# Hybrid decoder layer: turn, norm and spread inside the bursts of the next chunk, normaliser rows in another buffer pool, first loads of a recurrence two products sooner

## Chip, core and metric

The kernel runs on one core of a Trainium2 chip. The metric is device time in microseconds (us), from start to end of the program. Engines in the text: PE (TensorE, matmuls and transposes), DVE (VectorE), ACT (ScalarE), POOL (GpSimd) and SP (SyncE, which here issues all DMAs). Each engine works through its own list of instructions in order.

## The reference

One layer on a sequence of 2048 tokens with 1024 channels: a normalised input times one wide weight matrix; four mLSTM heads; two groups of a state-space scan; one output matrix over both; a residual sum and a last norm.

```python
h = rms_norm(x, norm_w[l])
proj = h @ w_in[l]
q, k, v, i_pre, f_pre, o_pre, z_m, z_s, xbc, dt_raw = jnp.split(proj, SPLIT_POINTS, axis=-1)
...
hm = mlstm_chunkwise(q.reshape(Bsz, T, M_HEADS, M_DQK), ...
hm = hm * lax.rsqrt(jnp.mean(hm * hm, axis=-1, keepdims=True) + EPS)
hm = hm.reshape(Bsz, T, M_WIDTH) * mlstm_norm_w[l].astype(f32)
hm = hm * jax.nn.sigmoid(o_pre.astype(f32)) * jax.nn.silu(z_m.astype(f32))
...
y = ssd_chunked(xs, dt, A, ...
y = y + d_skip[l].astype(f32)[:, None] * xs.astype(f32)
y = y.reshape(Bsz, T, S_WIDTH) * jax.nn.silu(z_s.astype(f32))
yg = y.reshape(Bsz, T, S_GROUPS, S_WIDTH // S_GROUPS)
yg = yg * lax.rsqrt(jnp.mean(yg * yg, axis=-1, keepdims=True) + EPS)
y = yg.reshape(Bsz, T, S_WIDTH) * ssd_norm_w[l].astype(f32)
mix = jnp.concatenate([hm, y], axis=-1).astype(dtype)
x = x + mix @ w_out[l]
...
return rms_norm(x, final_norm_w)
```

Both recurrences go in chunks of 128 tokens and carry a state (C for a head, H for a group) from chunk to chunk.

## The kernel before

**Products.** The two large matrix products are cut into 68 jobs. A job multiplies blocks by Strassen's scheme with seven products (R11, R21, T2, T3, T1, R22, T4 by the name of the right operand), and each product is 12 matmuls of 128x512 (L270), since every operand is split into a high and a low part. Two PSUM accumulators run through a job. The copy L289 by ACT takes the accumulator `pa` out after the product T1, and the product R22 then goes on accumulating in it, so R22 cannot start before L289 has ended; one product (R21 of the next job) stands between. Left operands are cast and split by ACT and DVE (L191, L192) a few products ahead. Between jobs of different stages the right operands are refilled from memory (L390).

**Stages and phases.** The input product has two stages (token halves s=0, s=1), each with six phases: heads h0, h1, h2, h3 and groups g0, g1 (order h0, g0, h1, h2, h3, g1; four jobs for a head, five for a group). Two output stages follow. The results of a phase are stored in memory (`hd`, `gd`), and the recurrence of a phase runs while the jobs of the next phase are computed.

**Recurrences.** A head's recurrence has eight chunks. For each chunk: `load` (L676 `hin`, L678 `nmi`, which holds the two rows of the normaliser broadcast to 128 partitions), `scores` (L686 to L704: masks and exponentials E and `w` from `nmi`, transposes of q, k, v on PE into `kw` and `vt`), `memory` (L714 to L735: three matmuls on PE; then square `sj` L731 and copy `mx` L732 on ACT; L733 to L735 on POOL scale `mx`), `gate` (L742 loads `g`) and `turn` (L751 transposes `mx` on PE, L752 multiplies by `g` on DVE, L753 stores to `mix`). A group's recurrence has, for each of its eight chunks, `decay` (L795 to L805), `tokens` (L813 to L829), `states` (L841 to L849), `update` (L857, L862), `outs` (L872 to L883: matmuls on PE, `y` on DVE, `q` on POOL), `norm` (L889 row sum on PE, `r` L891 on DVE, L892 and `dg` L894 on POOL) and `spread` (L901 on PE, L902 on DVE, then a store).

**Order.** PE's order is written by hand: the PE instructions of a recurrence stand in short bursts between two products. After each product `step()` runs: it takes the left operand's next piece, advances a clock by one tick, runs what `later(n, ...)` has put off by n ticks and what `at(...)` has planned, and lets the class Weave decide how many pieces of the recurrence (up to a `yield`) come next, so that NREC pieces are spread evenly over the products of the phase. Before, the turn of a chunk comes four ticks after its memory, the gate one tick after it, norm three and spread five ticks after the outputs. The order on DVE, ACT, POOL and SP is made by a scheduler from this program. `next_w` (from L516 on) prepares the output weights in the background of the second half, 64 pieces planned over 76 ticks; L532 loads a piece and L533 (ACT) scales it.

**Buffers.** Pools of equal buffers are shared by kinds of tiles: r2 (seven buffers: `hin`, `nmi`, `ea`, `xw`, `xdt`, `y`, `z` and others), r1 (six: `vt`, `mx`, `g`), r5 (nine: E, `qp`, `st`, `kw`, `bt`, `cbm`, `q`, `dg`).

Of the kernel before, what the change touches and what calls it, by code (L numbers as in the profile page):

```python
# [69 lines left out]
def hybrid_layer(ctx, tc, x, norm_w, w_in, b_igate, b_fgate, conv_w, conv_b, dt_bias,  # L70
# [30 lines left out]
        return mk([P, 1024], "t", 1, nm)  # L101

    def r2(nm, n=512):
        return mk([P, n], "r2", 7, nm)

    def r1(nm, n=NV):
        return mk([P, 272], "r1", 6, nm)[:, 0:n]

    def r5(nm, n=P):
        return mk([P, n], "r5", 9, nm)  # L110

    ident = cst.tile([P, P], F32, name="ident")
    make_identity(nc, ident)
# [235 lines left out]
    def out_pair(L, R, j, c):  # L349
        a, b = ot("oa"), ot("ob")  # L350
        gen = strassen(L, R, halves(a), halves(b), evac_copy)
        for _ in range(4):
            yield next(gen)
        xr = []
        for i in range(2):
            ct = c + i
            src = x[ct * P:(ct + 1) * P, :] if j == 0 else ymd[ct]
            if i == 0:
                t = tt_("xr")
                nc.sync.dma_start(t, src)  # L360
                xr.append((t[:, 0:TB], t[:, TB:]))
            else:
                t = [mk([P, 512], "hq", 3, "xr") for _ in range(2)]
                for k in range(2):
                    nc.sync.dma_start(t[k], src[:, k * TB:(k + 1) * TB])
                xr.append(t)
        yield from gen
        for i, t in enumerate((a, b)):
            ct = c + i
            for k in range(2):  # L370
                h = t[:, k * TB:(k + 1) * TB]
                (nc.vector if j and i else nc.gpsimd).tensor_add(h, h, xr[i][k])
            if j == 0:
                nc.sync.dma_start(ymd[ct], t)
                continue
            sq = mk([P, 1], "fsq", 2, "fsq")
            nc.scalar.activation(mk([P, DM], "r2", 7, "fj", BF16), t, AF.Square, accum_out=sq)
# [23 lines left out]
    def tok_norm(r0, nwb, t):  # L401
        if r0 is not None:
            nc.sync.dma_start(t, x[r0:r0 + P, :])
        ss = mk([P, 1], "ss", 4, "ss")
        jk = mk([P, DM], "r2", 7, "jk", BF16)
# [114 lines left out]
    def next_w():  # L520

        for j in range(2):
            for k in range(4):
                e = mk([P, HPG, P], "e4", 1, "we").rearrange("p a b -> p (a b)")
                q = {(0, 0): e[:, 0:TB], (1, 0): e[:, TB:]}
                for b in range(2):
                    q[b, 1] = mk([P, 6, P], "g3", 2, "wg").rearrange("p a b -> p (a b)")[:, 0:TB]
                for a in range(2):
                    r = j * 8 + a * 4 + k
                    for b in range(2):  # L530
                        u = q[a, b]
                        nc.sync.dma_start(u, w_out[r * P:(r + 1) * P, b * TB:(b + 1) * TB])  # L532
                        nc.scalar.activation(u, u, AF.Copy, scale=nwo[:, r:r + 1])  # L533
                yield

                def dst(o, i, v):
                    nc.sync.dma_start(wsd[j][o][:, i, k, :], v)

                yield from sums_out(q, dst)
# [128 lines left out]
    def rec_head(s, h):  # L668
# [3 lines left out]
        def load(n):  # L672
# [1 line left out]
            o = (b % 2) * TB + c * P  # L674
            t = r2("hin").rearrange("p (a l) -> p a l", a=4)
            nc.sync.dma_start(t, hd[s][h][:, 0:4, o:o + P])  # L676
            nmi = r2("nmi", 2 * P).rearrange("p (a l) -> p a l", a=2)
            nc.sync.dma_start(nmi, mrowd[b][:, h, c * P:(c + 1) * P].partition_broadcast(P))  # L678
            L["in", n] = (t, nmi)

# [26 lines left out]
        def memory(n):  # L707
# [9 lines left out]
            cps = rc_tile()  # L717
            nc.tensor.matmul(cps[:, 0:NV], lhsT=kw, rhs=vt, start=True, stop=True)
            if C is None:
                C = S["C"] = mk([P, NV + 14], "C", 1, "C")[:, 0:NV]  # L720
# [10 lines left out]
            nc.scalar.activation(mk([P, DV], "r5", 9, "sj", BF16), nps[:, 0:DV], AF.Square, accum_out=sq)  # L731
# [21 lines left out]
            nc.sync.dma_start(mixd[0][b * NCH + c][:, 2 * h:2 * h + 2, :], g)  # L753

        load(0)
        S["C"] = None
        if s:
            C = S["C"] = mk([P, NV + 14], "C", 1, "C")[:, 0:NV]
            nc.sync.dma_start(C, cd[h])
        yield  # L760
        scores(0)
# [1 line left out]
        load(2)  # L763
        yield
        for n in range(len(seq)):
            if n + 1 < len(seq):
                scores(n + 1)
            memory(n)
            if s == 0 and n + 1 == len(seq):
                nc.sync.dma_start(cd[h], S["C"])  # L770
            later(1, lambda n=n: gate(n))
            later(4, lambda n=n: turn(n))
            if n + 3 < len(seq):
                load(n + 3)
            yield

    def rec_group(s, g):
        seq = [(2 * s + i, c) for i in range(2) for c in range(NCH)]
# [125 lines left out]

        load(0)
        decay(0)
        S["H"] = None
        if s:
            H = S["H"] = mk([P, GW], "H", 1, "H")
# [3 lines left out]
        load(1)  # L913
        yield
        for n in range(len(seq)):
            states(n)
            yield
            update(n)
            if s == 0 and n + 1 == len(seq):
                nc.sync.dma_start(hdd[g], S["H"])  # L920
            outs(n)
            later(3, lambda n=n: norm(n))
            later(5, lambda n=n: spread(n))
            if n + 1 < len(seq):
                decay(n + 1)
                yield
# [1 line left out]
                if n + 2 < len(seq):  # L928
                    load(n + 2)
            yield  # L930

    def rec(s, ph):
        return rec_head(s, int(ph[1])) if ph[0] == "h" else rec_group(s, int(ph[1]))

    NREC = {"h": 10, "g": 25}

    class Weave:
        def __init__(self):
# [1 line left out]

        def set(self, g, n, total):
            self.finish()
            self.g, self.n, self.done, self.i, self.total = g, n, 1, 0, total
            next(g)

        def to(self):
# [87 lines left out]
    for n, jb in enumerate(jobs):  # L1034
# [35 lines left out]
        if more:  # L1070
            next(jobs[n + 1]["gen"])
            step(n + 1, "R21")
        next(g)
        step(n, "R22")
        next(g)
        step(n, "T4")
        next(g, None)
        if "s" in jb and (n + 1 == len(jobs) or jobs[n + 1].get("ph") != jb["ph"]):
            nxt = [k for k in jobs[n + 1:] if k.get("ph") == jobs[n + 1].get("ph") and k["stage"] == jobs[n + 1]["stage"]]
            wv.set(rec(jb["s"], jb["ph"]), NREC[jb["ph"][0]], 7 * len(nxt) if "s" in jobs[n + 1] else 42)  # L1080
            if jb["ph"] == "h1":
                bgq = next_w() if jb["s"] else next_h()
                total = 64 if jb["s"] else 84
# [32 lines left out]
```

## Time and profile before

| | |
|---|---|
| median of 3 runs | 1832.38 us |
| lowest, highest | 1822.41, 1832.39 us |
| the profiled execution | 1829.99 us |
| its span, first to last instruction | 1828.2 us |
| mean granted clock of PE in it | 0.966 |
| busy in the span: PE, DVE, ACT, POOL | 1679.5, 1308.7, 880.6, 450.2 us |

The profile is of one execution. Its span is 1.8 us shorter than that execution's time. An engine that is busy 92% of the span can still be the one that waits: what counts is what it waits for, and where. A matmul's duration on the page overlaps its successor's; the distance between two starts tells what one costs.

### The profile page before, as it was taken

What the parts mean: (1) busy time and instruction counts of PE and PEld (TensorE: products, weight loads), DVE (VectorE), ACT (ScalarE), POOL (GpSimd) and SP (SyncE); (2) the same over time, 40 slices, a digit from 0 to 9 for tenths busy, and PEclk for the clock granted to TensorE, in tenths of its full rate; (3) what the DMA queues carried; (4) which work ended last, traced back from release to release, by engine and by line L of the source; (5) the groups of instructions that cost most, each with busy time, mean ns of one, the idle gap of its engine ahead of it and who ended that gap; (6) DMA issues with size and microseconds to landing.
All of it is one profiled execution on the core that took longest, in us unless ns stands there. A gap on an engine that the chain in (4) does not pass through costs nothing.

```text
span 1828.2 us, 25057 instructions
## 1 busy us (share of the span) xinstructions
PE 1679.5 (92%) x8072; PEld 1357.2 (74%) x8072; DVE 1308.7 (72%) x2417; ACT 880.6 (48%) x1880; POOL 450.2 (25%) x629
## 2 busy tenths in 40 slices
PE   4999999999899798989899999898988889997997
PEld 4688887778788685767788777777776667776885
DVE  7677968877567693888675895655678578864775
ACT  5344644456566663434564444655565433332443
POOL 2000413332122131223121331202211144532222
PEclk9999999999999899999999999999999989998999
DMA  5245666668787689655575658888877976678543
GB/s 153 93 156 174 185 212 203 207 212 256 224 258 231 181 274 379 206 182 179 161 203 185 196 181 272 290 278 263 258 260 250 384 260 212 205 265 315 189 158 115
DMA packets 358323, 405.32 MB, mean 222 GB/s; under 512 B 30224, under 2 KB 284432, under 8 KB 352816
## 3 DMA queue, kind: packets, MB, share of 16 engines
q1 hardware_dynamic: 358192, 403.72, 68.1%
q8 instruction: 64, 1.05, 0.2%
q14 instruction: 67, 0.55, 0.1%
HBM read 251.40 MB, written 152.24 MB: 221 GB/s over the span
## 4 chain that ended last, share of the span: by engine, by line
PE 25%; DMA 15%; DVE 7%; issue 3%; ACT 2%; SPq 1%; POOL 1%; DVEq 0%; POOLq 0%; ACTq 0%
PE pj L270 21%; DMA E<-arow 1%; DMA we<-in_w_out 1%; DVE E L798 1%; DMA nmi<-mrow 1%; DMA mx<-mix 1%; DMA gin<-gd 1%; DMA ws1R<-hqh 1%; DMA T4l<-ws1T 1%; DMA ws0T<-hql 1%; DMA ws0R<-hqh 1%; DMA ws0T<-hqh 1%; DMA xr<-in_x 1%; DMA ws1T<-hqh 1%; PE rc L872 1%
## 5 line engine op out<-in xcount | busy, mean ns | idle before, releaser
L733 POOL TENSOR_SCALAR sq<-dn,sq 128x1 f32<-128x1 f32 x64 | 46.1, 720 | 624.9 <-ACT sj L731 477.8
L270 PE MATMUL pj<-R22h,S4h 128*128 128x512 f32 x272 | 119.7, 440 | 38.1 <-ACT ob L289 24.6
L270 PE MATMUL pj<-T2h,S2h 128*128 128x512 f32 x272 | 113.4, 417 | 11.6 <-ACT ca L276 9.3
L270 PE MATMUL pj<-T1l,S1h 128*128 128x512 f32 x272 | 107.3, 395 | 7.6 <-DMA T1l<-ws1T 7.2
L270 PE MATMUL pj<-R22l,S4h 128*128 128x512 f32 x272 | 113.1, 416 | 0.0
L270 PE MATMUL pj<-T4h,L22h 128*128 128x512 f32 x272 | 111.5, 410 | 1.4 <-DMA T4h<-ws1T 1.4
L270 PE MATMUL pj<-R11h,L11h 128*128 128x512 f32 x272 | 112.7, 414 | 0.0
L270 PE MATMUL pj<-R22h,S4l 128*128 128x512 f32 x272 | 112.7, 414 | 0.0
L270 PE MATMUL pj<-T2l,S2h 128*128 128x512 f32 x272 | 109.0, 401 | 4.0 <-DMA T2l<-hsT 3.3
L270 PE MATMUL pj<-T1h,S1h 128*128 128x512 f32 x272 | 111.0, 408 | 1.4 <-ACT cbt L283 1.4
L270 PE MATMUL pj<-R21h,L12h 128*128 128x512 f32 x272 | 110.1, 405 | 0.0
L270 PE MATMUL pj<-T3h,S3h 128*128 128x512 f32 x272 | 109.3, 402 | 0.0
L270 PE MATMUL pj<-T2h,S2l 128*128 128x512 f32 x272 | 108.6, 399 | 0.0
L270 PE MATMUL pj<-T1h,S1l 128*128 128x512 f32 x272 | 107.2, 394 | 1.3 <-DVE S1l L192 1.3
L270 PE MATMUL pj<-T4l,L22h 128*128 128x512 f32 x272 | 106.6, 392 | 1.9 <-DMA T4l<-ws1T 1.9
L270 PE MATMUL pj<-T4h,L22l 128*128 128x512 f32 x272 | 106.7, 392 | 0.0
L270 PE MATMUL pj<-R11h,L11l 128*128 128x512 f32 x272 | 106.6, 392 | 0.0
L270 PE MATMUL pj<-R11l,L11h 128*128 128x512 f32 x272 | 106.5, 391 | 0.0
L270 PE MATMUL pj<-T3h,S3l 128*128 128x512 f32 x272 | 106.3, 391 | 0.0
L270 PE MATMUL pj<-R21l,L12h 128*128 128x512 f32 x272 | 106.3, 391 | 0.0
L270 PE MATMUL pj<-R21h,L12l 128*128 128x512 f32 x272 | 106.3, 391 | 0.0
L270 PE MATMUL pj<-T3l,S3h 128*128 128x512 f32 x272 | 106.3, 391 | 0.0
(330 smaller groups left out, 4697.4 us busy)
## 6 DMA issues: line engine op xcount, KB each, us to landing
wa<-in_w_in SPq DMA_DIRECT2D x52, 512.0 KB, 6.2
s<-sum SPq DMA_DIRECT2D x52, 512.0 KB, 5.3
hd<-ob SPq DMA_DIRECT2D x32, 512.0 KB, 3.8
E<-arow SPq DMA_DIRECT2D x32, 512.0 KB, 5.2
hin<-hd SPq DMA_DIRECT2D x64, 256.0 KB, 4.7
mx<-mix SPq DMA_DIRECT2D x32, 512.0 KB, 4.9
wb<-in_w_in SPq DMA_DIRECT2D x26, 512.0 KB, 4.2
sum<-ls SPq DMA_DIRECT2D x26, 512.0 KB, 4.6
```

The costliest lines, as they stand in the source:

```text
L270: nc.tensor.matmul(ps, lhsT=l[:, k, :], rhs=r[:, k, :], start=start and k + n == 0, stop=k == 3 and n == 2, skip_group_check=True)
L733: nc.gpsimd.tensor_scalar(sq, dn, DV * EPS, sq, op0=ALU.mult, op1=ALU.add)
L798: nc.vector.tensor_scalar(E[:, r, :], E[:, r, :], G["cum"][:, c, k:k + 1], 0.0, op0=ALU.subtract, op1=ALU.min)
L872: nc.tensor.matmul(yps[o:o + HD, (r // 2) * P:(r // 2 + 1) * P], lhsT=xdt[:, r * HD:(r + 1) * HD], rhs=E[:, r, :], start=True, stop=True, ...
```

## The change

- `turn(n - 1)` is called at the front of burst n, ahead of `scores(n + 1)` and `memory(n)`; `gate(n)` is called in burst n itself. The last chunk's turn has a piece of its own.
- `norm(n - 1)` is called ahead of `states(n)`, `spread(n - 1)` ahead of `update(n)`.
- Both recurrences have more pieces, and NREC goes from 10 to 12 and from 25 to 29.
- The recurrence is created and its first piece run ahead of the last job's step R22 (before: after its step T4); that piece now has the first load alone.
- `nmi` is taken from r1 (six to eight buffers); r2 goes from seven to six, r5 from nine to eight. The head's state C shares a buffer with the group's state H.
- `next_w` waits three pieces between loads and scaling, and has 80 pieces over the same ticks.

```diff
-            nmi = r2("nmi", 2 * P).rearrange("p (a l) -> p a l", a=2)
+            nmi = r1("nmi", 2 * P).rearrange("p (a l) -> p a l", a=2)
...
         for n in range(len(seq)):
+            if n:
+                turn(n - 1)
             if n + 1 < len(seq):
                 scores(n + 1)
             memory(n)
             if s == 0 and n + 1 == len(seq):
                 nc.sync.dma_start(cd[h], S["C"])
-            later(1, lambda n=n: gate(n))
-            later(4, lambda n=n: turn(n))
             if n + 3 < len(seq):
                 load(n + 3)
+            gate(n)
             yield
+        turn(len(seq) - 1)
+        yield
...
         for n in range(len(seq)):
+            if n:
+                norm(n - 1)
             states(n)
             yield
+            if n:
+                spread(n - 1)
             update(n)
             if s == 0 and n + 1 == len(seq):
                 nc.sync.dma_start(hdd[g], S["H"])
             outs(n)
-            later(3, lambda n=n: norm(n))
-            later(5, lambda n=n: spread(n))
...
-    NREC = {"h": 10, "g": 25}
+    NREC = {"h": 12, "g": 29}
...
-                        nc.scalar.activation(u, u, AF.Copy, scale=nwo[:, r:r + 1])
-                yield
+                for _ in range(3):
+                    yield
+                for a in range(2):
+                    r = j * 8 + a * 4 + k
+                    for b in range(2):
+                        nc.scalar.activation(q[a, b], q[a, b], AF.Copy, scale=nwo[:, r:r + 1])
...
+        ends = "s" in jb and (not more or jobs[n + 1].get("ph") != jb["ph"])
+        if ends:
+            pre = rec(jb["s"], jb["ph"])
+            next(pre)
         next(g)
         step(n, "R22")
```

PE in a head's recurrence, before: a burst between the products R22 and T4. `hin` holds q, k, v of a chunk; rc is a PSUM buffer of the recurrences, pj one of the products.

```order
L270 MATMUL pj<-R22h,S4l 128x512
L694 MATMUL rc<-hin 128x128
L696 MATMUL rc<-ident,hin 128x128 x3
L714 MATMUL rc<-vt,st 128x258
L716 MATMUL rc<-C,qp 128x258
L718 MATMUL rc<-vt,kw 128x258
L270 MATMUL pj<-T4h,L22h 128x512
```

The turn of the chunk before stands by itself one product later, between T4 and T2:

```order
L270 MATMUL pj<-T4l,L22h 128x512
L270 MATMUL pj<-T4h,L22l 128x512
L751 MATMUL rc<-ident,mx 128x128 x2
L270 MATMUL pj<-T2h,S2h 128x512
L270 MATMUL pj<-T2l,S2h 128x512
```

After, both are one burst (here between T4 and T2), with the turn (L755, before L751) ahead:

```order
L270 MATMUL pj<-T4h,L22l 128x512
L755 MATMUL rc<-ident,mx 128x128 x2
L698 MATMUL rc<-hin 128x128
L700 MATMUL rc<-ident,hin 128x128 x3
L718 MATMUL rc<-vt,st 128x258
L720 MATMUL rc<-C,qp 128x258
L722 MATMUL rc<-vt,kw 128x258
L270 MATMUL pj<-T2h,S2h 128x512
```

The turn of a chunk has moved from four products behind its memory to two or three, and, but for a head's last, no longer stands alone.

PE in a group's recurrence, before: between two products stands the spread (L901) of one chunk with the first matmuls of another; a product later come a norm (L889), an update and the outputs.

```order
L270 MATMUL pj<-R22h,S4l 128x512
L901 MATMUL rc<-dg,ones 128x128
L845 MATMUL rc<-gin,H 128x128 x4
L270 MATMUL pj<-T4h,L22h 128x512
...
L270 MATMUL pj<-T4h,L22l 128x512
L889 MATMUL rc<-ones,q 128x1
L857 MATMUL rc<-xw,bt 128x512
L872 MATMUL rc<-E,xdt 64x128 x8
L270 MATMUL pj<-T2h,S2h 128x512
```

After, in three bursts of the four recurrences the norm (L897) and the spread (L909) of one chunk stand in one:

```order
L270 MATMUL pj<-T2h,S2l 128x512
L897 MATMUL rc<-ones,q 128x1
L853 MATMUL rc<-gin,H 128x128 x4
L909 MATMUL rc<-dg,ones 128x128
L865 MATMUL rc<-xw,bt 128x512
L880 MATMUL rc<-E,xdt 64x128 x8
L270 MATMUL pj<-T3h,S3h 128x512
```

In the usual place a product lies between norm and spread; there were three.

SP at the end of phase g1 of the second half, before: the first load of its recurrence (`gin`, L788) behind the refills of R22 and T4 for the next stage (h and l are the high and low parts) and two stores. Numbers behind names tell buffers in memory apart.

```order
L390 DMA R22h<-ws0R_186 128x2048
L390 DMA R22l<-ws0R_186 128x2048
L346 DMA gd_1_111<-oa 128x1024
L346 DMA gd_1_111<-ob 128x1024
L390 DMA T4h<-ws0T_187 128x2048
L390 DMA T4l<-ws0T_187 128x2048
L788 DMA gin<-gd_1_111 128x6x128
```

After:

```order
L757 DMA mix_15_127<-g 128x256
L796 DMA gin<-gd_1_111 128x6x128
L803 DMA E<-arow_150 128x1024
L390 DMA R22h<-ws0R_186 128x2048
L390 DMA R22l<-ws0R_186 128x2048
L346 DMA gd_1_111<-oa 128x1024
L346 DMA gd_1_111<-ob 128x1024
```

The load has moved ahead of four refills and two stores; a store of the head before it (`mix`) stands ahead of it.

## Rows read from the trace of the kernel before

**Rows 1.** the page, part 1: busy time, share and instructions of each engine

```profile
PE 1679.5 (92%) x8072; PEld 1357.2 (74%) x8072; DVE 1308.7 (72%) x2417; ACT 880.6 (48%) x1880; POOL 450.2 (25%) x629
```

**Rows 2.** waits of PE: waiting tile, line <- awaited: us, times, longest

```profile
PE pj L270 <- ACT ob L289: 24.6, 10, 5.9
PE pj L270 <- ACT cbt L289: 13.4, 5, 5.4
PE rc L813 <- DMA gin<-gd: 12.0, 1, 12.0
...
PE rc L872 <- DVE y L902: 3.9, 4, 1.7
...
PE rc L889 <- POOL q L883: 2.9, 4, 1.0
...
PE rc L751 <- POOL mx L735: 2.0, 1, 2.0
```

**Rows 3.** timeline of PE: start us, us, instruction; around a turn alone

```profile
198.92 0.39 PE L270 MATMUL pj<-R11h,L11l 128*128 128x512 f32 x1
...
199.60 0.39 PE L270 MATMUL pj<-T1l,S1h 128*128 128x512 f32 x1
```

**Rows 4.** timeline of PE: a turn within a burst

```profile
207.57 0.38 PE L751 MATMUL rc<-ident,mx 128*128 128x128 f32 x2
207.79 0.39 PE L694 MATMUL rc<-hin 128*128 128x128 f32 x2
```

**Rows 5.** timeline of SP's queue: start and us of issue

```profile
1450.96 0.86 SPq L390 DMA_DIRECT2D T4h<-ws0T  x1
...
1452.62 0.71 SPq L788 DMA_DIRECT2D gin<-gd  x1
```

**Rows 6.** timeline of PE, the last group recurrence opens; in brackets idle before

```profile
1467.55 0.79 PE L813 MATMUL rc<-gin 128*128 128x128 f32 x2 [12.01 <-DMA gin<-gd]
...
1473.47 0.48 PE L270 MATMUL pj<-R22l,S4h 128*128 128x512 f32 x1
```

**Rows 7.** a stretch: busy us by engine; behind POOL the granted clock

```profile
1468.50:1473.00 4.50, 4.50 (x14) 3.68 (x13) 3.73 (x12) 2.43 (x5) 0.00 (x0) 0.50 1.05 363
```

**Rows 8.** timeline of ACT, scaling of a w_out row

```profile
1216.84 0.72 ACT L533 ACTIVATE we<-we,nwo 128x512 f32<-128x512 f32 x1 [5.84 <-DMA we<-in_w_out]
```

**Rows 9.** timeline of PE, the product behind it

```profile
1219.83 0.80 PE L270 MATMUL pj<-R22h,S4h 128*128 128x512 f32 x1 [4.37 <-ACT ob L289]
```

**Rows 10.** POOL's last step: ns min/median/max, first and last start

```profile
L735 POOL TENSOR_SCALAR mx<-mx,sq x64: 932/1040/4320, 182.0 to 1440.4; 128x256 f32<-128x256 f32 x64
```

**Rows 11.** timeline of PE, memory of a chunk, seventh head

```profile
1260.37 0.60 PE L718 MATMUL rc<-vt,kw 128*128 128x258 f32 x2
```

**Rows 12.** timeline of ACT behind it

```profile
1266.36 0.30 ACT L690 ACTIVATE w<-nmi,u 128x1 f32<-128x1 f32 x1 [4.04 <-DMA nmi<-mrow]
```

**Rows 13.** timeline of POOL behind that

```profile
1270.76 1.63 POOL L735 TENSOR_SCALAR mx<-mx,sq 128x256 f32<-128x256 f32 x1
```

**Rows 14.** waits of ACT

```profile
ACT w L690 <- DMA nmi<-mrow: 91.7, 36, 5.5
```

**Rows 15.** DMA issues: count, KB each, median us to landing

```profile
nmi<-mrow SPq DMA_DIRECT2D x64, 128.0 KB, 6.0
```

**Rows 16.** timeline of PE, outputs of a group chunk

```profile
1080.72 1.09 PE L872 MATMUL rc<-E,xdt 128*64 128x128 f32 x16 [0.27 <-DVE y L902]
```

**Rows 17.** timeline of POOL, its q and its dg

```profile
1087.61 0.79 POOL L883 TENSOR_TENSOR q<-z 128x128 f32<-128x128 f32 x1
...
1096.97 0.61 POOL L894 TENSOR_SCALAR dg<-ident,r 128x128 f32<-128x128 f32 x1
```

**Rows 18.** timeline of PE, its norm

```profile
1091.98 0.35 PE L889 MATMUL rc<-ones,q 128*128 128x1 f32 x2
```

**Rows 19.** timeline of DVE, its r

```profile
1096.08 0.15 DVE L891 TENSOR_SCALAR r<-rc 128x1 f32<-128x1 f32 x1
```

**Rows 20.** a group recurrence as one stretch, columns as above

```profile
281.00:376.00 95.00, 89.33 (x512) 71.14 (x511) 85.01 (x171) 40.21 (x84) 36.77 (x40) 0.98 0.64 195
```

More of the change, by code (lines that the diff above doesn't have):

```diff
@@ L103, in r2 @@
     def r2(nm, n=512):
-        return mk([P, n], "r2", 7, nm)
+        return mk([P, n], "r2", 6, nm)
     def r1(nm, n=NV):
-        return mk([P, 272], "r1", 6, nm)[:, 0:n]
+        return mk([P, 272], "r1", 8, nm)[:, 0:n]
     def r5(nm, n=P):
-        return mk([P, n], "r5", 9, nm)
+        return mk([P, n], "r5", 8, nm)
     ident = cst.tile([P, P], F32, name="ident")
@@ L376, in out_pair @@
             sq = mk([P, 1], "fsq", 2, "fsq")
-            nc.scalar.activation(mk([P, DM], "r2", 7, "fj", BF16), t, AF.Square, accum_out=sq)
+            nc.scalar.activation(mk([P, DM], "r2", 6, "fj", BF16), t, AF.Square, accum_out=sq)
             nc.gpsimd.tensor_scalar(sq, sq, 1.0 / DM, EPS, op0=ALU.mult, op1=ALU.add)
@@ L404, in tok_norm @@
         ss = mk([P, 1], "ss", 4, "ss")
-        jk = mk([P, DM], "r2", 7, "jk", BF16)
+        jk = mk([P, DM], "r2", 6, "jk", BF16)
         nc.scalar.activation(jk, t, AF.Square, accum_out=ss)
@@ L719, in memory @@
             if C is None:
-                C = S["C"] = mk([P, NV + 14], "C", 1, "C")[:, 0:NV]
+                C = S["C"] = mk([P, GW], "H", 1, "C")[:, 0:NV]
                 nc.vector.tensor_copy(C, cps[:, 0:NV])
@@ L730, in memory @@
             sq = mk([P, 1], "sq", 3, "sq")
-            nc.scalar.activation(mk([P, DV], "r5", 9, "sj", BF16), nps[:, 0:DV], AF.Square, accum_out=sq)
+            nc.scalar.activation(mk([P, DV], "r5", 8, "sj", BF16), nps[:, 0:DV], AF.Square, accum_out=sq)
             nc.scalar.copy(mx, nps[:, 0:DV])
@@ L755, in rec_head @@
         load(0)
+        yield
         S["C"] = None
         if s:
-            C = S["C"] = mk([P, NV + 14], "C", 1, "C")[:, 0:NV]
+            C = S["C"] = mk([P, GW], "H", 1, "C")[:, 0:NV]
             nc.sync.dma_start(C, cd[h])
@@ L770, in rec_head @@
                 nc.sync.dma_start(cd[h], S["C"])
-            later(1, lambda n=n: gate(n))
-            later(4, lambda n=n: turn(n))
             if n + 3 < len(seq):
                 load(n + 3)
+            gate(n)
             yield
+        turn(len(seq) - 1)
+        yield
     def rec_group(s, g):
@@ L906, in rec_group @@
         decay(0)
+        yield
         S["H"] = None
@@ L930, in rec_group @@
             yield
+        yield
+        norm(len(seq) - 1)
+        yield
+        spread(len(seq) - 1)
+        yield
     def rec(s, ph):
         return rec_head(s, int(ph[1])) if ph[0] == "h" else rec_group(s, int(ph[1]))
-    NREC = {"h": 10, "g": 25}
+    NREC = {"h": 12, "g": 29}
     class Weave:
@@ L942, in set @@
             self.finish()
-            self.g, self.n, self.done, self.i, self.total = g, n, 1, 0, total
+            self.g, self.n, self.done, self.i, self.total = g, n, 2, 0, total
             next(g)
@@ L1077, in hybrid_layer @@
         next(g, None)
-        if "s" in jb and (n + 1 == len(jobs) or jobs[n + 1].get("ph") != jb["ph"]):
+        if ends:
             nxt = [k for k in jobs[n + 1:] if k.get("ph") == jobs[n + 1].get("ph") and k["stage"] == jobs[n + 1]["stage"]]
-            wv.set(rec(jb["s"], jb["ph"]), NREC[jb["ph"][0]], 7 * len(nxt) if "s" in jobs[n + 1] else 42)
+            wv.set(pre, NREC[jb["ph"][0]], 7 * len(nxt) if "s" in jobs[n + 1] else 42)
             if jb["ph"] == "h1":
                 bgq = next_w() if jb["s"] else next_h()
-                total = 64 if jb["s"] else 84
+                total = 80 if jb["s"] else 84
                 for i in range(total):
```

## Prediction

> **What bounds the kernel now.** I read the first part of the page, then the waits of TensorE (PE), then the stretches around the longest of them. PE is busy 92% of the span, no other engine over 72% [rows 1], and its work is the same in both kernels. So the time can move only by what PE does not work, 1828.2 - 1679.5 = 149 us. The list of PE's waits says for what [rows 2]. Three kinds matter here. 38 us are waits for ScalarE's (ACT) copy L289. One wait of 12.0 us is for the load `gin` that opens a group recurrence. Seven rows of 2.0 to 4.1 us, 22.7 us together, are short waits inside the recurrences; those for y, q and mx stand for them. The rest is refills and stores that the change leaves alone.
>
> **What a break in the product stream costs.** The change merges small PE steps into the bursts, so first the price of a small step that stands alone. In [rows 3] the last matmul of a product starts at 198.92, then comes a turn, and the second matmul of the next product starts at 199.60. Matmuls of a product follow each other every 0.227 us (a whole product takes 2.72); without the turn there would be two such steps, 0.45 us, and there are 0.68: alone the turn costs 0.23 us. Within a burst a turn starts at 207.57 and the scores behind it at 207.79: 0.22 us [rows 4]. So merging saves 0.01 us a time at most. The order has 257 breaks before and 190 after; 67 x 0.01 is below 1 us. **Merging as such is worth nothing**; I put it at 0.
>
> **The first loads.** In the last group phase SP issues `gin` at 1452.62, behind T4h and T4l (2 MB, from 1450.96 on) [rows 5] and, ahead of these, two stores and two R22 refills. PE gets it at 1467.55, after 12.01 us idle [rows 6]; then the granted clock is 0.50, the 1.2 GHz level [rows 7], up to the product matmul at 1473.47. Ten product matmuls stand before that one, at 0.44 us each instead of 0.23. That is 12.0 + 10 x (0.44 - 0.23) = 14.1 us. After the change SP has `gin` ahead of R22h, R22l, two stores and both T4 refills, about 5 MB less before it, and the first products that use it come a step later. I take the whole 14 (bounds 0 and 14).
>
> **The scaling of w_out.** ACT waits 5.84 us for `we` at 1216.84 [rows 8], and the copy L289 stands behind it in its order; PE then starts R22 at 1219.83 after 4.37 us idle [rows 9], and the ten matmuls behind it go at the lower clock as in [rows 7]. Three yields of distance are about three products, 8.2 us, more than 5.84. So -4.4 - 2.1 = -6.5 us (bounds 0 and 6.5). The cover: had the load taken over 8 us, the wait would stay.
>
> **The turn.** Before, a turn stands four products (11 to 14 us) after the memory step whose result it needs, and PE waited for it once, 2.0 us [rows 2]. After, 44 of 64 stand two products later, which is 5.4 us (6.4 with the burst), the others three, 8.2 us. What the chain needs is read from pairs of memory matmul and POOL's last step, 64 of each; the first of the latter starts at 182.0, the last at 1440.4 [rows 10]. The time between their ends is 2.5 us at least, 7 in the middle, 18.3 at most. Chunk 3 of the seventh head shows why: the memory matmul starts at 1260.37 [rows 11], ACT sits 4.04 us for `nmi` until 1266.36 [rows 12] and squares only then, POOL ends at 1270.76 + 1.63 = 1272.39 [rows 13], 11.4 us. With the latencies of before, 39 of 64 turns would be late by 125 us in all; if a wait once paid lets the chain catch up for the rest of a head, the worst turn of each head counts, 45 us. The same reading made of before with its own slack gives 13.5 us where the trace has 2.0, so it overstates: by that ratio 125 becomes 19. I choose 20, near that end, because the order of ACT after the change has no `w` between `vt` and `sj` any more (11 chunks had one). Bounds 0 and 45.
>
> Whether ACT's lag goes is decided by `nmi`. ACT waits 91.7 us for it, 36 of 64 times [rows 14]. It lands 6.0 us after its issue in the middle [rows 15]. After the change the first three of a head are issued far earlier. From the fourth on its buffer comes free only when a turn is done, one burst (about 7.5 us) ahead of its use. On SP it stands behind the store of the turn's result, which waits for VectorE's (DVE) multiplication; with the 6.0 us that fills the 7.5, so I expect some of these waits to stay.
>
> The Trainium skill ("DMA: Bandwidth & Descriptors", section "Anatomy of one DMA — SWDGE (gpsimd) path") fits a transfer as 2.0 us plus bytes over 436 KB per us, by which 128 KB would take an estimated 2.3 us, and `nmi` would be there in time. The trace has 6.0, on SP's queue and beside other traffic, and I go by it.
>
> **Norm and spread.** A chunk's row sum goes L872, `y`, POOL's `q`, norm. For one chunk L872 starts at 1080.72 and takes 1.09 [rows 16], q ends at 1087.61 + 0.79 [rows 17], 6.6 us later; over 32 chunks 4.2 to 11.0. Norm then needs DVE's `r` and POOL's `dg` before the spread: norm at 1091.98 [rows 18], `r` only at 1096.08 [rows 19] behind six other DVE instructions, `dg` done at 1096.97 + 0.61 [rows 17], 5.3 us; over 32 chunks 1.6 to 10.2. Before, the slack was about 10 and 8.6 us. After, norm has 6.2 us in the usual burst, 3.5 in the six that hold two steps, 8.9 in the last group; the spread has 3.6, and 0.9 where both stand in one burst. Unrelieved this is 40 + 70 = 110 us; one worst chunk for each group is 20 + 20 = 40. By the ratio of the turn it is 16. DVE is what is late, and it has little room: in one group recurrence it is busy 85 of 95 us [rows 20], in the other three 86 to 87%, and the same eight chunks now fit in 21 products instead of 24. So I take 30, the upper half. Bounds 6 (even the shortest chains, 4.2 and 1.6, miss the 3.5 and 0.9 of nine steps by 0.7 each) and 40.
>
> The buffers I put at 0: `nmi` leaves the pool r2 with the buffer that r2 loses, r5 has one of nine less and its tiles wait for DVE rather than for a buffer, and C takes H's place only when the group recurrence before it has ended. If a missing r5 buffer did hold up a chunk, it would be one more late `dg` or `kw`, within the bounds above.
>
> What these waits replace: a PE that waits at the turn or norm finds y, E, vt, xdt ready. Of the 22.7 us of such waits I take off half, 11 (bounds 0 and 23).
>
> **The sum**, against the profiled execution (1829.99 us, of which the span is 1828.2; the median of the runs is 1832.38): +20 + 30 - 11 - 14.1 - 6.5 = +18, so 1848 us.
>
> **The rivals.**
> - *Faster.* ACT no longer lags, because the first `nmi` are early and `w` stands better in its order. The turn's chain is then near its shortest, 2.5 us, under the 5.4 it has, and norm and spread pay the least, 6. -14.1 - 6.5 - 11 + 6 gives -26: 1804 us. It decides as soon as the mx chain stays below 5.4 us. For it: the short chains exist (15 of 64 took 2.5 to 4.2 us). Against it: chunks with nothing between `vt` and `sj` still had 6.6 us in the middle. By the rule of the skill named above, `nmi` would never be late, and this would be the case.
> - *No change.* The turns are free, but norm and spread wait as summed: 30 - 11 - 20.6 = -2: 1828 us. For it: DVE's load; against it: the chain of 11.4 us [rows 11 to 13].
> - *Much slower.* Nothing is replaced and the worst chunk counts in full: 45 + 40 - 20.6 = +64: 1894 us. For it: the late `r` [rows 19]; against it: a wait lets the other engines catch up.
>
> **How the numbers follow.** Chances: the sum 0.42 (1836 to 1870 for itself), faster 0.25, no change 0.18, much slower 0.15. About 1% is what a measurement of this kernel can tell from no change; that is 1814 to 1851. The sum's case lies half below 1851. Faster: most of the second case, 0.23. Slower: 0.21 + 0.15 = 0.36. Same: the rest, 0.41. The range 1800 to 1885 leaves out the lower part of the faster case (about 0.1) and most of the much slower one (about 0.1).
>
> **What would show it.** The 12.0 us before `gin`'s first matmul and the 4.4 us at the L289 copy behind `we` should be gone. The list of PE's waits should have L755 <- POOL mx with about 20 us in many short pieces, L897 <- POOL q and L909 <- POOL dg with about 30, and y, E, vt, xdt with less than before. If mx does not show up, the faster case or no change is right. Wrong in kind would be a new wait for a refill (R22, T4) that the early loads push back, or L289 waits that grow because ACT blocks on a later `nmi`.

## The result, and the profile after

The changed kernel takes 1971.5 us (median of 4 runs, 1962.7 to 1976.6) where the kernel before takes 1832.4: a ratio of 1.077 (95% interval 1.071 to 1.083). The prediction put the time at 1848 with a range up to 1885, and gave slower a chance of 0.36. The loss is 139 us, not 16.

The page of the changed kernel, first part, and its clock (columns as in [rows 1]; core, span, mean granted clock of PE):

```profile
PE 1726.3 (87%) x8072; PEld 1382.4 (70%) x8072; DVE 1310.4 (66%) x2417; ACT 882.0 (45%) x1880; POOL 475.5 (24%) x629
```

```profile
core 0: 1974.5 us, clock 0.946
```

The span is 146 us longer. PE has the same 8072 instructions but is busy 1726.3 us instead of 1679.5, and its idle share went from 1828.2 - 1679.5 = 149 us to 1974.5 - 1726.3 = 248 us. So 99 us are idle time, and for 47 us more PE is busy with the same matmuls: the mean granted clock fell from 0.966 to 0.946. DVE and ACT are busy for as long as before (POOL's spans are 25 us longer).

What PE waits for in the changed kernel (columns as in [rows 2]):

```profile
PE rc L755 <- POOL mx L739: 69.5, 32, 7.6
PE rc L909 <- POOL dg L902: 57.0, 21, 7.0
PE rc L897 <- POOL q L891: 25.1, 8, 6.6
...
PE pj L270 <- ACT cbt L289: 7.2, 3, 2.8
...
PE pj L270 <- ACT ob L289: 7.1, 5, 2.9
PE rc L569 <- DMA R22h<-hsR: 5.9, 1, 5.9
```

The three rows at the top are the three steps that were moved: turn (mx), spread (dg), norm (q), 151.6 us together; before they were 2.0, 4.1 and 2.9. Against [rows 2], the waits at L289 went from 38.0 to 14.3, and the 12.0 us for `gin` are gone. R22h and others are new.

**One late spread.** PE, POOL and DVE between the norm of a chunk and its spread in the first group (timeline of the changed kernel; start us, us, instruction, idle before). This is the longest wait for a spread:

```profile
373.76 0.28 PE L897 MATMUL rc<-ones,q 128*128 128x1 f32 x2
...
382.08 0.80 PE L909 MATMUL rc<-dg,ones 128*128 128x128 f32 x2 [7.05 <-POOL dg L902]
```

```profile
373.25 1.66 DVE L806 TENSOR_SCALAR E<-E,cum 128x128 f32<-128x128 f32 x8 [0.78 <-DMA E<-arow]
374.83 1.22 DVE L333 SCALAR_TENSOR_TENSOR ob<-oa,ob 128x1024 f32<-128x1024 f32 x1
375.96 0.28 DVE L835 TENSOR_TENSOR cbm<-rc,tri 128x128 f32<-128x128 f32 x1
376.16 1.86 DVE L334 SCALAR_TENSOR_TENSOR ob<-tz,ob 128x1024 f32<-128x1024 f32 x1
377.95 1.21 DVE L837 TENSOR_TENSOR E<-E,cbm 128x1024 f32<-128x1024 f32 x1
379.08 0.68 DVE L192 TENSOR_TENSOR L12l<-wa,L12h 128x512 fp32r<-128x512 f32 x1
379.69 0.14 DVE L899 TENSOR_SCALAR r<-rc 128x1 f32<-128x1 f32 x1
```

```profile
379.91 0.57 POOL L900 TENSOR_TENSOR r<-r,mhalf 128x1 f32<-128x1 f32 x1 [2.97 <-DVE r L899]
380.58 1.45 POOL L902 TENSOR_SCALAR dg<-ident,r 128x128 f32<-128x128 f32 x1
```

The step on DVE that the spread needs takes 0.14 us, but it stands behind six kinds of other work, and DVE is busy with these from 373.25 to 379.69 without a stop. That place is given by DVE's order, and a wait of PE changes nothing in it. PE sits still for 7.05 us. The other late spreads are alike: in all 21 of them together 67 us pass from the end of the norm on PE to `r` on DVE, and DVE is busy with other instructions for 65 of these.

**One late turn.** Chunk 4 (counted from 0) of the sixth head: memory, then ACT up to the square, then POOL, then the turn:

```profile
1274.39 0.60 PE L722 MATMUL rc<-vt,kw 128*128 128x258 f32 x2
```

```profile
1276.33 0.29 ACT L694 ACTIVATE w<-nmi,u 128x1 f32<-128x1 f32 x1 [2.28 <-DMA nmi<-mrow]
1276.53 0.60 ACT L191 CAST S3h<-s 128x512 fp32r<-128x512 f32 x1
1277.04 0.58 ACT L289 COPY ob<-pj 128x512 f32<-128x512 f32 x1
1281.29 0.72 ACT L538 ACTIVATE wg<-wg,nwo 128x512 f32<-128x512 f32 x1 [3.67 <-DMA wg<-in_w_out]
...
1282.41 0.39 ACT L735 ACTIVATE sj<-rc 128x256 bf16<-128x256 f32 x1
```

```profile
1284.02 1.47 POOL L739 TENSOR_SCALAR mx<-mx,sq 128x256 f32<-128x256 f32 x1
```

```profile
1285.54 0.69 PE L755 MATMUL rc<-ident,mx 128*128 128x128 f32 x2 [4.85 <-POOL mx L739]
```

ACT waits for `nmi` and then for a piece of w_out ahead of the square. The chain takes 10.5 us, about as long as the late one of before (11.4 in [rows 11 to 13]), and PE is at the turn 5.7 us after the memory. Of the 32 late turns, 14 have such a wait of ACT for a load between memory and square, 7 of them for `nmi`; in the others the chain was late without one.

### The profile page after: what moved, and what is told of

Read it like the earlier page. It is cut to its first block, busy times and chain, and to the rows that moved or that the text cites. A ratio compares the mean times of both kernels' runs of the same rounds, so it can differ in the third digit from the quotient of the medians.

```text
span 1974.5 us, 25154 instructions
## 1 busy us (share of the span) xinstructions
PE 1726.3 (87%) x8072; PEld 1382.4 (70%) x8072; DVE 1310.4 (66%) x2417; ACT 882.0 (45%) x1880; POOL 475.5 (24%) x629
## 5 line engine op out<-in xcount | busy, mean ns | idle before, releaser
L737 POOL TENSOR_SCALAR sq<-dn,sq 128x1 f32<-128x1 f32 x64 | 55.4, 866 | 696.7 <-ACT mx L736 312.1
L270 PE MATMUL pj<-R22h,S4h 128*128 128x512 f32 x272 | 114.7, 422 | 18.1 <-ACT cbt L289 7.2
```

What stands on the lines that cost most here:

```text
L270: nc.tensor.matmul(ps, lhsT=l[:, k, :], rhs=r[:, k, :], start=start and k + n == 0, stop=k == 3 and n == 2, skip_group_check=True)
```

## The experiments

The change splits into five parts that can each be done or undone: turn (with gate), norm and spread, first loads, scaling of w_out, buffers. All ratios are against the kernel before, run on the same chip with them (medians 1829.6 to 1832.1). The waits in the last column are those of one profiled execution each.

| run | what is changed against before | median us | ratio, 95% interval | PE waits for mx; q and dg, us |
|---|---|---|---|---|
| the changed kernel | all | 1971.5 | 1.077, 1.071 to 1.083 | 69.5; 82.1 |
| e1 | all but the turn | 1952.4 | 1.064, 1.059 to 1.069 | 4.3; 78.9 |
| e2 | all but norm and spread | 1907.9 | 1.042, 1.039 to 1.045 | 59.9; 12.3 |
| e8 | all but the buffers | 1919.8 | 1.049, 1.045 to 1.053 | 43.7; 71.6 |
| e16 | all, r2 with seven buffers | 1939.8 | 1.058, 1.056 to 1.060 | 59.1; 66.1 |
| e3 | loads, scaling, buffers | 1884.6 | 1.029, 1.026 to 1.032 | 1.4; 13.3 |
| e4 | loads, scaling | 1839.8 | 1.006, 1.004 to 1.009 | 0.9; 16.5 |
| e5 | buffers | 1867.2 | 1.020, 1.016 to 1.024 | 2.0; 6.5 |
| e6 | buffers, r2 with seven | 1846.0 | 1.009, 1.006 to 1.013 | 2.0; 7.0 |
| e7 | turn | 1850.9 | 1.011, 1.006 to 1.016 | 44.1; 9.0 |
| e9 | scaling | 1830.8 | 0.999, 0.997 to 1.002 | 2.0; 8.4 |
| e10 | loads | 1850.9 | 1.011, 1.008 to 1.014 | 3.3; 15.7 |
| e11 | turn merged, but later, NREC 12 | 1833.5 | 1.002, 0.999 to 1.004 | 0; 11.4 |
| e12 | norm sooner, spread late, NREC 27 | 1865.4 | 1.017, 1.012 to 1.022 | 4.1; 21.3 |
| e13 | loads, weave as before | 1837.8 | 1.004, 1.003 to 1.005 | 4.1; 12.2 |
| e14 | load of the last phase | 1829.5 | 0.999, 0.997 to 1.000 | 2.0; 7.2 |
| e15 | norm, spread, weave as before | 1868.9 | 1.020, 1.018 to 1.022 | 2.0; 52.5 |
| e17 | r2 eight, r5 eight | 1824.8 | 0.998, 0.995 to 1.000 | 2.2; 4.9 |
| e18 | r2 eight, r1 five | 1823.0 | 0.997, 0.994 to 0.999 | 2.2; 5.7 |

The kernel before has 2.0 and 7.0 in the last column. The theory that I started from: all of the loss lies in the moved steps, whose chains miss their new slack. Its rivals: the buffers make every chain late wherever its consumer stands; or DVE bounds the group recurrences, and their denser weave costs.

### Each moved step put back (e1, e2, e3), loads and scaling alone (e4)

e1, from the changed kernel (e2 does the same for norm, three ticks, and spread, five; e3 both):

```diff
-            if n:
-                turn(n - 1)
...
+            later(1, lambda n=n: gate(n))
+            later(4, lambda n=n: turn(n))
             if n + 3 < len(seq):
                 load(n + 3)
-            gate(n)
             yield
-        turn(len(seq) - 1)
-        yield
...
-    NREC = {"h": 12, "g": 29}
+    NREC = {"h": 11, "g": 29}
```

> The changed kernel with turn and gate put off by four and one ticks again, all else as changed (one piece less in NREC for a head). Theory (the turn is too early for its chain, 69.5 us of PE waits, and each wait brings a stretch at the 1.2 GHz level): the 69.5 us and about 69.5/152 of the 47 us of added PE busy time, 21 us, go: 1971 - 91 = 1880 us, PE waits for mx under 5 us. Rival (the buffers and the other engines' order make every chunk late, wherever the turn stands): the wait moves to the scores or the memory of a later burst, and the time stays above 1940 us.

> The changed kernel with norm and spread put off by three and five ticks again, turn as changed. Theory (norm and spread are too early): the 82 us of waits for q and dg fall to the 7 us of before, with 47 x 82/152 = 25 us of busy time: 1971 - 75 - 25 = 1871 us. Rival (DVE bounds the group recurrences): less than half of the 75 us comes back, above 1915 us.

> The changed kernel with turn, gate, norm and spread all put off again: only the early first loads, the distance in the scaling of w_out and the buffers stay changed. Theory (all of the loss lies in the moved steps): the sum of the two effects, 1971 - 91 - 100 = 1780 us at best; by the prediction's own terms the early loads and the scaling give -21 us against before, 1812 us. Rival (nmi in the smaller pool costs by itself): above 1840 us.

e4 is the kernel before with the two hunks on `next_w` and on `ends`, `pre` and the first `yield` of both recurrences (NREC one up for each).

> The kernel before with the early first load and the later scaling of w_out alone. Theory (both terms of the prediction hold): 12.0 us before gin and the 4.4 us behind we are gone with their slow matmuls, 1832 - 21 = 1812 us. Rival (something else takes their place, such as a refill that now comes later): 1825 to 1840 us, with a new wait on R22 or T4.

The waits for mx went in e1, as the theory said, but only 19 us of time with them, so that the time is where the rival had it. Two things were missing from the 91 us. The waits at L289 came back (19.5 and 15.6 us, against 7.1 and 7.2 in the changed kernel): 65 us of waits for mx had stood in for 21 us of others. The likely reason is that ACT gets ready for L289 while PE waits at a turn. And the 21 us of slow matmuls did not go at all:

```profile
core 0: 1950.6 us, clock 0.946
```

PE is busy 1730.3 us in e1, not less than the 1726.3 of the changed kernel, at the same clock. In e2 64 us come back, less than expected as well; 23.5 of these are busy time (1702.8 us in the profiled execution, with a clock of 0.961; the four have 0.954 to 0.961). The surprise is e3: with all steps back where they were, 55 us of loss are left, while e4 is at +10. What lies between e3 and e4 is the buffers.

### The buffers (e5, e6, e16), the turn alone (e7), all but the buffers (e8)

e5 is the kernel before with the buffers of the change (pool sizes, `nmi` in r1, C in H's place); e6 is e5, and e16 the changed kernel, with r2 at seven:

```diff
-        return mk([P, n], "r2", 6, nm)
+        return mk([P, n], "r2", 7, nm)
```

> The kernel before with the buffers of the change alone: nmi from r2 to r1, r1 six to eight, r2 seven to six, r5 nine to eight, C in H's place. Theory A (the pools cost by themselves; the two earlier runs that differ in them alone, 1884.6 and 1839.8, say 45 us): 1830 + 45 = 1875 us, with the loss in the group recurrences, where no nmi lives and r2 is simply one buffer short: ACT's wait for ea near 60 us instead of 40. Theory B (the pools matter only when turns and first loads have moved): within 10 us of before, 1820 to 1840 us.

> As the run with the buffers alone, but r2 keeps its seven buffers. If the missing r2 buffer in the group recurrences is what costs, this is back at 1830 to 1840 us; if nmi in r1 (its buffer comes free only after a turn) or the r5 buffer costs, it stays with the run that has six, near 1875 us.

> The changed kernel with seven buffers in r2 again. If the missing r2 buffer costs the same here as it did alone (1867 against 1846 us), 1971 - 21 = 1950 us, ACT's wait for ea back near 45 us from 67. If its cost was only part of the waits for q and dg (which then hide it), above 1963 us.

> The kernel before with turn and gate moved into the next burst, all else as before, nmi in r2. Theory A (too little slack whatever the pools): PE waits for mx near 60 us and, with the slow matmuls behind them and less waiting at L289, 1830 + 20 to 25 = 1853 us, as the same step gave on the changed pools (19 and 23 us). Theory B (nmi that can only be loaded when a turn is done makes ACT late, so the waits feed themselves): with nmi in r2 the mx waits stay under 25 us and the time within 10 us of before.

> The changed kernel with the buffers of before: all moved steps, early first loads, later scaling. If the parts add up, 1971 - 45 = 1926 us. If the short pools are what makes the moved steps late, much less, below 1890 us, with the waits for mx, q and dg at half of their 152 us or under.

ACT's waits for the loads of `ea` (a group's, in r2) and for `nmi` (a head's) in e5, then in e6:

```profile
ACT w L690 <- DMA nmi<-mrow: 129.7, 46, 5.8
...
ACT ea L805 <- DMA ea<-arow: 62.4, 23, 7.1
```

```profile
ACT w L690 <- DMA nmi<-mrow: 131.1, 50, 5.3
...
ACT ea L805 <- DMA ea<-arow: 46.0, 22, 4.7
```

Two costs stand apart here. The buffer that r2 lost costs 21 us (1867 to 1846), and ACT's wait for `ea` shows it: 62 us with six, 46 with seven, 40 before. In the changed kernel the same buffer is worth 32 us (e16). So e6 lies between its two expectations, and the 32 us are more than the 21 expected of e16. The other 14 us (e6 against before) probably go with `nmi` in r1: ACT waits 131 us for it, 92 before [rows 14]. r5 and the shared C changed in e6 too, and no run has `nmi` in r1 alone; but e17 below has r5 at eight and e11 and e17 have the shared C, and neither is slower than the kernel before by more than 3 us.

The turn alone costs 19 us, with 44 us of waits for mx even with `nmi` in r2:

```profile
PE rc L751 <- POOL mx L735: 44.1, 20, 5.5
```

Its waits at L289 are 16.0 us, against 38.0 before. With everything but the buffers the waits for mx are 43.7 us (e8), with r2 at seven 59.1 (e16), in the changed kernel 69.5. So the buffers make these waits longer by 26 us, about 10 by the one of r2 and the rest by `nmi`, r5 and C together, but they do not cause them. All but the buffers is at +88; the buffers cost 52 us in the changed kernel and 35 alone.

### The scaling (e9) and the first loads (e10, e13, e14)

> The kernel before with the later scaling of w_out alone. Theory A (the prediction's term): the 4.37 us behind the copy L289 at the eighth head's end and its slow matmuls go, nothing else moves: 1830 - 6.5 = 1824 us. Theory B (three more pieces hold the buffers of the loaded rows longer, so the next loads come later and ACT waits elsewhere): 1830 to 1840 us, ACT's waits for we and wg not below their 18 us.

In e9 the 4.4 us are still there. ACT at the scaling, the product behind it, and SP at the load:

```profile
1219.62 0.72 ACT L538 ACTIVATE we<-we,nwo 128x512 f32<-128x512 f32 x1 [6.95 <-DMA we<-in_w_out]
```

```profile
1221.38 0.79 PE L270 MATMUL pj<-R22h,S4h 128*128 128x512 f32 x1 [4.43 <-ACT ob L289]
```

```profile
1214.02 2.21 SPq L532 DMA_DIRECT2D we<-in_w_out  x2
```

The rows of before had 5.84 us [rows 8] and 4.37 us [rows 9]. SP issues the load at 1214.02, 5.6 us ahead of its use; in the kernel before it issued it at 1211.05, 5.8 us ahead. Three more pieces between the two lines of the program made no distance between load and scaling on the chip; why SP's order has the load later too is open.

e13 and e14 hold the weave to its old number of pieces; e14 does the early piece for the last phase alone:

```diff
+        ends = "s" in jb and (not more or jobs[n + 1].get("ph") != jb["ph"])
+        if ends:
+            pre = rec(jb["s"], jb["ph"])
+            if jb["s"] == 1 and jb["ph"] == "g1":
+                next(pre)
...
+            if not (jb["s"] == 1 and jb["ph"] == "g1"):
+                next(pre)
+            wv.set(pre, NREC[jb["ph"][0]], 7 * len(nxt) if "s" in jobs[n + 1] else 42)
```

> The kernel before with the early first load of a recurrence alone. Theory A: the 12.0 us before gin go with their slow matmuls and nothing takes their place: 1830 - 14 = 1816 us. Theory B (the refills that now stand behind the early loads on SP come late, and what follows a phase's end moves with them): new waits for R22 and T4 of 7 to 10 us with slow matmuls behind each, 1835 to 1845 us.

> The kernel before with every recurrence's first load two products sooner, but the number of pieces and the start of the weave as before (in the run with the first loads alone a recurrence had one piece more to fit into the same products). Theory A (the denser weave is what cost): the loss of 20 us goes, and the 12 us before gin are gained: 1816 to 1826 us. Theory B (the refills behind the early loads are late): R22 waits of 10 us or more stay with their slow matmuls, 1835 to 1848 us.

> As the run before it, but only the last group recurrence of the second half has its first load early, the one where PE waited 12 us. Theory A: -12.0 and 2 us of slow matmuls less, against 4 to 6 us of a later R22 refill: 1820 to 1826 us, under before. Theory B (the wait only moves to the refills behind): 1828 to 1834 us, no change.

In e14 PE no longer waits for `gin`. SP's queue there, then PE at the refill of the next stage:

```profile
1453.38 0.32 SPq L261 DMA_DIRECT2D mx<-mix  x1
...
1454.69 0.55 SPq L789 DMA_DIRECT2D gin<-gd  x1
...
1457.21 0.55 SPq L390 DMA_DIRECT2D R22h<-ws0R  x1
```

```profile
1465.91 0.76 PE L270 MATMUL pj<-R22h,S4h 128*128 128x512 f32 x1 [4.34 <-DMA R22h<-ws0R]
1468.24 0.80 PE L270 MATMUL pj<-R22l,S4h 128*128 128x512 f32 x1 [1.57 <-DMA R22l<-ws0R]
```

SP is one queue, and it is held up ahead of both, for 10.8 us at a load of left operands (L261) that waits for DVE. What is issued first pushes back the rest. `gin` comes in time, but not alone: a group's first piece has `decay(0)` too, so the loads of `E` and `ea` also go ahead of the refill. SP issues R22h 3.8 us behind the L261 load, where it was 1.4 us before (1447.39 and 1448.76; all of e14 is about 6 us later at this point), and PE waits for it. From the last matmul of R21 to the first of T2 it is 18.7 us in e14 and 22.4 before. So about 4 of the 14 us are gained at this place, and the waits for the refills, with the slow matmuls behind them, take the rest. In the time of the whole kernel nothing can be told from none (e14); with all first loads early it is 7 us worse (e13), and with one piece more in the same products 20 us (e10). The 13 us between e10 and e13 are no fixed price of that piece: e4 has it too, with the scaling beside it, and costs 10 us in all. Why is open.

### Merging with the old slack (e11), norm and spread apart (e12), at the old density (e15)

e11, from the kernel before, with r1 at seven buffers, C in H's place and NREC at 12 for a head:

```diff
+            if n > 1:
+                turn(n - 2)
             if n + 1 < len(seq):
                 scores(n + 1)
             memory(n)
...
-            later(1, lambda n=n: gate(n))
-            later(4, lambda n=n: turn(n))
             if n + 3 < len(seq):
                 load(n + 3)
+            gate(n)
             yield
+        turn(len(seq) - 2)
+        yield
+        turn(len(seq) - 1)
+        yield
```

> The kernel before with the turn of the chunk before last at the front of each burst, so merged as in the change, but four or five products behind its memory (r1 seven buffers instead of six, C in H's place). Theory A (merging is worth nothing and the slack is all): PE waits for mx stay at or under 4 us and the time is that of before, 1825 to 1835 us, 20 us under the run with the turn one burst sooner. Rival (a stop in the product stream costs more than its rows show): below 1820 us. Third (a turn in a burst costs whatever its slack): near 1850 us.

The time is that of before. Merging neither gains nor costs; of two kernels that both merge the turn, the one that lets it wait four or five products is 17 us faster than the one that lets it wait two or three (e7; r1, C and NREC differ between these two as well).

e12 puts the norm where the change has it, and the spread three ticks behind it, with NREC at 27; e15 has both where the change has them, NREC at 25 and the last two steps by `later`, so that eight chunks take 24 products as before:

```diff
             if n:
                 norm(n - 1)
+                later(3, lambda n=n - 1: spread(n))
```

> The kernel before with the norm one product sooner, as in the change, but the spread three products behind the norm. Theory A (the chain to q and the chain to dg each miss their slack by themselves): waits for q of 10 to 25 us stay, those for dg fall under 10 us, and of the 59 us that norm and spread cost together about a third is left: 1845 to 1855 us. Theory B (the two feed each other: a wait at the norm moves the spread's chain and the other way round): the time is within 10 us of before, with q under 8 us.

> The kernel before with norm and spread where the change has them, two products behind the outputs and one behind the norm, but the eight chunks in 24 products as before, not in 21. Theory A (the short slack costs): waits for q and dg of 40 us or more, 1860 to 1890 us. Theory B (the denser weave costs, since DVE has 12 us of work for each chunk): q and dg below 25 us, 1835 to 1850 us.

PE in e15:

```profile
PE rc L901 <- POOL dg L894: 44.6, 20, 4.8
...
PE rc L889 <- POOL q L883: 7.9, 6, 4.0
```

In e12 dg is as good as gone from the waits (1.5 us), q has 19.8 and `xdt` 16.5 (the profiled execution was the slowest of four, 1876 us); it costs 35 us, more than half of the 59 that were to be split and more than either theory had. In e15, at the old density, the short slack costs 38 us, with most of the waits at dg. So slack and not density is the larger part; e12, with its 27 pieces, holds some of both. The rest up to 59 (which is e8 less e7 and e4: 88 - 19 - 10) goes with the denser weave or with the other parts together; no run here tells these apart.

### More r2 instead of less (e17, e18)

```diff
-        return mk([P, n], "r2", 7, nm)
+        return mk([P, n], "r2", 8, nm)
...
-        return mk([P, 272], "r1", 6, nm)[:, 0:n]
+        return mk([P, 272], "r1", 5, nm)[:, 0:n]
...
-            C = S["C"] = mk([P, NV + 14], "C", 1, "C")[:, 0:NV]
+            C = S["C"] = mk([P, GW], "H", 1, "C")[:, 0:NV]
```

> The kernel before with the buffers the other way round: r2 eight instead of seven, paid for by r5 eight instead of nine and C in H's place; nmi stays in r2. Theory A (r2 is short before the change too, in head recurrences where hin and nmi alone take up to eight): ACT's wait for nmi falls from 92 to below 70 us, the waits at L289 from 38 to below 25 us, 1815 to 1825 us, under before. Theory B (seven are enough, only the loss of one costs, or r5 costs as much): 1826 to 1836 us.

> As the run beside it, but the buffer for r2 comes out of r1 (five instead of six), r5 keeps nine. If r1 (vt, mx, g) has room to spare: the same time as the run beside it, within 5 us. If not: waits of scores or gate for a buffer that a turn frees, 1835 to 1850 us.

ACT's wait for `nmi` in e18:

```profile
ACT w L690 <- DMA nmi<-mrow: 63.2, 28, 4.7
```

An eighth r2 buffer takes a third off that wait (92 to 63 us, in e17 as well), and e18 is the one kernel here that is clearly under the one before, by 0.35% (interval 0.14 to 0.57%); for e17 the interval reaches 0. The waits at L289 hardly moved (37.6 against 38.0 us) and rose in e17 (42.5, where below 25 was expected), so it is not by them that it gains; through what it does was not tried. The profiled execution of e18 is the fastest of its twelve (1813.6 us), so its waits are read at the favourable end. e17 has r5 at eight and e18 at nine, and they take the same time within 2 us (r1 differs as well): what one r5 buffer less costs can't be seen here.

## Why the prediction was wrong, point by point

- **Bound, and merging worth nothing: right.** PE had the same instructions, and e11 shows merging at its price of nothing. That the time can move only by what PE does not work held for 99 us; the rest came by its clock.
- **The turn, +20 (bounds 0 and 45): mis-sized.** It was 69.5 us of waits in the changed kernel and 44.1 alone. The step that failed is "if a wait once paid lets the chain catch up". The time from memory to `mx` is 6.9 us in the middle before and 6.3 after, over 64 chunks each, although PE waited at 32 of them. In the seventh head PE waited at six chunks in a row, and each of their chains still took 6.3 to 9.4 us. It is no lag that a wait works off: the square on ACT stands behind other work, and in 14 of the 32 behind a load, anew. The longest wait of each head, which was to be all, adds up to 32 us of the 69.5. The 69.5 lie between the sum with relief, 45, and the one without, 125. The ratio 2.0 to 13.5, which argued for the low end, came from one wait; and where `w` no longer stands between `vt` and `sj`, it stands ahead of both, as the late turn above shows, so the square is still behind it. That the turn alone cost 19 us of time (e7) is luck: 42 us more of waits for mx, less 22 us at L289 that no term had.
- **`nmi`: some waits stay, right; they grew.** ACT's wait for it went from 91.7 to 119.7 us. The shortest load of `nmi` took 4.7 us before and 4.8 after. The estimate of 2.3 us from the Trainium skill ("DMA: Bandwidth & Descriptors", section "Anatomy of one DMA — SWDGE (gpsimd) path"), whose fit is stated for transfers that GpSimd issues, is not seen in either trace, on SP's queue.
- **Norm and spread, +30 (bounds 6 and 40): the same step failed.** 82 us of waits, where the unrelieved sum was 110 and the relieved one 40; 38 us of time alone at the old density (e15). The chain to dg has a middle of 5.2 us before and 5.4 after, against a slack of 3.6 us in the usual burst. That DVE is what is late was right.
- **The clock: missing.** The sum counted slow matmuls where waits go, and none where waits come. PE's busy time grew by 47 us, a third of the loss. It goes with norm and spread more than with the turn: put back, norm and spread take 23.5 us of it away (e2), the turn nothing (e1), and the turn alone adds 5 us (1684.5 us in e7).
- **What the waits replace, -11: right.** The rows for y, E, vt and xdt among the 22.7 us had 13.7 us before and have 2.3 after. What no term had is that the waits at L289 fell by 24 us too; e1 brings 21 of these back.
- **First loads, -14: wrong.** The wait at `gin` went as foretold, but its place was taken by the refills behind it (e14), which the last lines of the prediction name as a possible error, and all first loads early cost 7 us (e13), 20 with an extra piece in the weave (e10).
- **Scaling, -6.5: wrong.** The step that failed is that three pieces of the program are three products between load and scaling. The load came later too (e9: 5.6 us ahead of its use, 5.8 before).
- **Buffers, 0: wrong.** "`nmi` leaves the pool r2 with the buffer that r2 loses" holds for heads alone. In a group recurrence no `nmi` lives, and r2 was simply one short. 35 us alone, 52 in the changed kernel. That the r5 buffer and the shared C would cost nothing fits e17 and e11.

The chance of 0.15 for "much slower" was the case that came, and it went past its price of 1894 us: that took the worst chunk only (85 us of waits, where 151.6 were measured), still had 20.6 us off for loads and scaling, and nothing for clock and buffers.

The parts alone add up to 19 (turn) + 38 (norm and spread) + 10 (loads and scaling) + 35 (buffers) = 102 of 139 us. The rest shows only when they come together: the buffers cost 17 us more beside the moved steps than alone, and the other parts together 21 us more than one by one (88 against 67). By what is open.

## What to carry to other kernels

Before a consumer is moved closer to its producer, take the whole distribution of the chain's length and count every instance that misses the new slack; do not assume that a wait relieves later ones, since a link that stands behind other work in its engine's queue stands there again in the next chunk. Ask of a wait on the engine that sets the time whether slower matmuls come behind it, and which other waits it takes away. A pool shared by two phases must be counted in the phase that does not use the tile that left it, and a load that is brought forward on a single queue pushes back those that now stand behind it.

## What the runs showed of the hardware

In the changed kernel as a whole, 99 us of added idle time of PE came with 47 us of added busy time for the same matmuls. By the mean clocks this is the lower level: at 0.946 over 1974.5 us an estimated 2 x 0.054 x 1974.5 = 213 us are spent at 0.50, at 0.966 over 1828.2 us 124, and half of the difference is about 44 us. It is no fixed rate. The turn alone added 18.5 us of idle time and 5 of busy time (e7), and its going from the changed kernel took 28 us of idle time away and none of the busy time (e1):

```profile
core 0: 1851.7 us, clock 0.966
```

The four executions of e7 have clocks of 0.962 to 0.966 and those of the kernel before beside them 0.966 to 0.969; e1 has 0.944 to 0.953 and the changed kernel 0.946 to 0.951. Why the waits of norm and spread cost more of the clock than those of the turn is open.

Behind one spread, that at 363.43 in the changed kernel, which PE had waited 3.63 us for, the granted clock was 0.50 for the whole stretch:

```profile
363.50:366.50 3.00, 3.00 (x10) 1.50 (x12) 1.15 (x2) 0.00 (x0) 0.00 (x0) 0.50 0.00 0
```

That is the 1.2 GHz level, after 3.63 us without a matmul.
